# A hybrid decoder layer on one core: eight instead of six fast pairs per pass of the last product, and gate biases that arrive by DMA

## The chip, the cores and the metric

The kernel runs on one core of one Trainium2 chip. The metric is device time in microseconds (us). Before the change three runs took 1597.12, 1597.80 and 1598.16 us; the median is 1597.8. One more execution was recorded by the hardware profiler; every row of a profile in this document comes from such a recording.

Five engines matter: TensorE (PE) multiplies matrices, and its weight loads are listed apart as PEld; VectorE (DVE) and ScalarE (ACT) work element by element; GpSimd (POOL) is nearly unused; SyncE (SP) issues the DMA transfers. Each engine takes its own instructions in order.

## The reference

The reference is one layer of a decoder trunk over 256 tokens of width 2048, in f32. From the conditioning vector c it forms six modulation vectors:

```python
mod = jax.nn.silu(c) @ w_ada[l] + b_ada[l]
shift1, scale1, gate1, shift2, scale2, gate2 = jnp.split(mod[:, None, :], N_MOD, axis=-1)
h = rms_norm(x, norm1_gain[l]) * (1 + scale1) + shift1
x = x + gate1 * mixing_sublayer(h, ...)      # three token mixers, one output product
h = rms_norm(x, norm2_gain[l]) * (1 + scale2) + shift2
x = x + gate2 * swiglu(h, w_ffn_in[l], w_ffn_out[l])
```

`swiglu` splits `h @ w_ffn_in` into two halves of width 5632, takes `silu(gate) * up`, and multiplies by `w_ffn_out` (5632 x 2048). This product with `w_ffn_out` is the last product of the kernel. The change touches it and the biases `b_ada` of the two gates.

## The kernel before

**Three matmuls per product.** Every f32 factor is split into a high part (a cast to fp32r, written `hi`, `whi`) and a low part (the rest, `lo`, `wlo`). `mm3` (L163) issues hi x hi, hi x lo and lo x hi into one PSUM bank; each is a matmul of 128x128 by 512 columns. ACT casts the high part and DVE subtracts for the low part. For weights that happens in `load_weights` (L146, L158, L159) and in `load_pair` (L1269, L1276, L1277), out of pools of four buffers each: `raw`, `whi`, `wlo`. One buffer holds two 128-row chunks of 512 columns.

**Units and pairs.** The feed-forward network runs in 11 units of 512 columns. `act[e]` holds the high and low part of unit e, transposed: four chunks of 128 rows (k) by 256 tokens. The last product runs over 44 chunks, which is 22 pairs of chunks, by four column blocks of 512. Pass one (`OUT_A`) forms column blocks 0 and 1 over all 22 pairs. Pass two (`OUT_B`) forms blocks 2 and 3 over a part of the pairs, and `block` calls add the rest, with the last block's end split by token half so that little is left behind the final matmul.

**Ordinary and fast pairs.** For a pair, two chunks by two token halves meet two chunks by two column blocks: eight block products, 24 matmuls. `fast_products` (L1284 and on) can instead form a pair by seven block products (a Strassen-like scheme, 21 matmuls). It then needs sums of the left factors (`sums_of_unit`, L1427 and on; `sums_of`, L1251) and of the weights (`load_pair`: one 1024-wide and five 512-wide subtractions more than for an ordinary pair, L1277 and L1280, four of them in the buffers with the tags AR0 and AR1). Seven products land in eight banks: the four accumulators and four shared ones, which are added to the accumulators after the last fast pair of a pass (`merge`, L1311, out of the sums L1352 to L1355). Before the change six pairs of each pass are fast: pairs 8 to 13, whose left factors belong to units 4, 5 and 6. The tuples `OUT_A` and `OUT_B` list the order as (pair, fast); `hooks` says before which position the sums of a unit are written out, and at which position `flush` completes all background work.

**The gates.** A modulation vector is a product with `w_ada` that DVE forms: for each of 16 chunks and two halves a tile of 128x1024 is loaded (L375, SP), and one instruction adds weight times silu(c) to an accumulator (`ada_mac`: L286 for the first chunk, a multiplication; L288 for the others). `rows_of` (L965 and on) then adds the bias to row 0 of each quarter of the accumulator (DMA L970, DVE add L971), splits the quarters into high and low parts (L980, L981) and multiplies them by a matrix of ones on PE (L985, L986), which sums over the partitions and leaves the gate in every row. This is background work: a generator from which `tick` takes a step at a given rate per two chunks of a `block`, `RATE_FFN` = 0.65 in the feed-forward network and 2.5 in the last product. Gate 2 starts with unit 8. A multiply-add is issued three steps after its load, and is queued on DVE behind the last weight split that the code has written out by then (`issue_after`); within a block that is the block's last split, so these instructions run in bursts towards the end of a block. Gate 1 is formed in the same way during the mixing sub-layer, in tiles with the tags T4 and T5.

**What sets the order.** The code is written in one order, and a scheduler sorts the instructions of each engine by priority and by the time at which its own model finds them ready. Work inside `prio()` counts as 4000 instructions earlier; all weight loads and splits are such work, and the sums of left factors are not. On the chip each engine then keeps the order it was given. A tile with one buffer (AR0, AR1, KC, ada) is free for its next owner only when every reader of the old contents is done.

Of the kernel before, what the change touches and what calls it, by code (L numbers as in the profile page):

```python
# [10 lines left out]
F32 = mybir.dt.float32  # L11
F32R = mybir.dt.float32r
# [5 lines left out]
P = 128  # L18
# [14 lines left out]
RATE_IN, RATE_MID, RATE_FFN = 0.8, 0.6, 0.65  # L33
RATE_OUT = 2.5
LOOK = 3
# [41 lines left out]
def trunk(ctx: ExitStack, tc: tile.TileContext, I, out):  # L77
# [205 lines left out]
    def ada_mac(acc, raw, k):  # L283
        c = csil[:, k : k + 1]
        if k == 0:
            nc.vector.tensor_scalar(acc, raw, c, None, op0=ALU.mult)  # L286
        else:
            nc.vector.scalar_tensor_tensor(acc, raw, c, acc, op0=ALU.mult, op1=ALU.add)  # L288
# [69 lines left out]
    def mac():  # L358
        acc, j, k, raw, done = macs.pop(0)
        with tc.issue_after(state["split"].ins):  # L360
            ada_mac(acc[j], raw, k)
        if done is not None:
            after.append(done)

    def ada_segment_steps(acc, seg, done):


        for k in range(KC):
            for j in range(2):
                while len(macs) >= len(ring["tags"]):  # L370
                    mac()
                raw = araw([P, 2 * NB])
                c0 = seg * D + j * 2 * NB
                with prio():
                    nc.sync.dma_start(raw, w_ada[k * P : (k + 1) * P, c0 : c0 + 2 * NB])  # L375
                macs.append((acc, j, k, raw, done if (k, j) == (KC - 1, 1) else None))
                yield
# [587 lines left out]
    def rows_of(name, seg, acc):  # L965

        quarters = [a[:, c : c + NB] for a in acc for c in (0, NB)]
        for j, q in enumerate(quarters):
            br = scr([1, NB])
            nc.sync.dma_start(br, I["b_ada"][:, seg * D + j * NB : seg * D + (j + 1) * NB])  # L970
            nc.vector.tensor_add(q[0:1, :], q[0:1, :], br)  # L971
            yield
# [21 lines left out]
    def background():  # L994
        for seg in (SEG_SHIFT2, SEG_GATE1, SEG_SCALE2):
            if seg == SEG_GATE1:
                acc = [S(f"T{4 + j}", [P, 2 * NB]) for j in range(2)]
                yield from ada_segment_steps(acc, seg, rows_of("gate1", seg, acc))
# [241 lines left out]
    def gate2_bg():  # L1240
        acc = halves(S("ada", [P, D]))
        yield from ada_segment_steps(acc, SEG_GATE2, rows_of("gate2", SEG_GATE2, acc))
        yield from last_macs()
# [180 lines left out]
    CUT = KF - 14  # L1424
    w_fo = I["w_ffn_out"]
    out_sums = {}

    def sums_of_unit(n):
# [6 lines left out]
        hi, lo = (S(f"H{2 + 2 * n + i}", [P, 4, 2, P], F32R) for i in range(2))  # L1435
        nc.scalar.copy(hi, sf)
        nc.vector.tensor_tensor(lo, sf, hi.bitcast(F32), op=ALU.subtract)
        for m in range(2):
            out_sums[2 * e + m] = [(hi[:, j, m, :], lo[:, j, m, :]) for j in range(4)]
# [3 lines left out]
    hooks = {at: (lambda n=n: sums_of_unit(n)) for n, at in enumerate((1, 2, 4))}  # L1443
    hooks[7] = flush
# [7 lines left out]
    REST = 2 * len(OUT_B)  # L1452
    block(o[0], act_at, w_fo, REST, KF, 2 * NB, go_on=True, seeded=True)
# [5 lines left out]
    block(pss, act_at, w_fo, REST, CUT, n * NB, go_on=True, more=True, seeded=True)  # L1459
# [42 lines left out]
```

## Time and profile before

| | |
|---|---|
| median of three runs | 1597.8 us |
| the profiled execution, its time | 1597.22 us |
| its span, first to last instruction | 1595.4 us |
| granted TensorE clock | 1.000 |
| PE / DVE / ACT / POOL busy | 1582.0 / 1275.5 / 837.6 / 5.3 us |
| DMA, mean | 248 GB/s |
| last product, first matmul to last | 1352.9 to 1591.0 us |

Times within the profile count from the first instruction. A row of a timeline gives start, duration, engine, source line, operation, what is written and read (buffer numbers left out), the shape, and in brackets how long the engine had been idle before and whom it had waited for. "L166" is line 166 of the kernel; the lines of a helper are shared by all who call it. Neighbouring rows of one kind can be merged. A matmul's listed duration is longer than its distance to the next, because matmuls are pipelined; a few matmul records can be missing. A row of a group gives the busy time in all, the mean of one in nanoseconds, and the idle time before.

### The profile page before, as it was taken

The numbers are of one execution on the slowest core, as the hardware profiler recorded it, in microseconds if no ns is written. First come the engines' busy times: TensorE is split into PE (matmuls) and PEld (weight loads), VectorE is DVE, ScalarE is ACT, GpSimd is POOL, SyncE is SP. The second block draws the span as 40 slices with busy tenths as digits, with TensorE's granted clock in tenths as the row PEclk, the third lists the DMA queues.
The fourth block names the chain that finished last, engine by engine and source line by source line (L and its number), as shares of the span: only waits on it lengthen the run. The fifth ranks groups of instructions, "written<-read, shape, count | busy, mean of one in ns | idle before, by whom it ended". The sixth has DMA issues, their size and how long they took to land.

```text
span 1595.4 us, 20167 instructions
## 1 busy us (share of the span) xinstructions
PE 1582.0 (99%) x7272; PEld 1308.2 (82%) x7272; DVE 1275.5 (80%) x1523; ACT 837.6 (53%) x1184; POOL 5.3 (0%) x14
## 2 busy tenths in 40 slices
PE   8999999999999999999999999999999999999998
PEld 7878888888888888888887888888888888778887
DVE  6889995888878787878756688888887677988884
ACT  5654449775754434444446655555454443554552
POOL 1000000000000000000000000000000000000000
PEclk9999999999999999999999999999999999999999
DMA  9999997667778889989766466556657889667664
GB/s 339 365 326 320 332 302 245 214 189 257 247 258 280 297 301 314 311 289 310 228 192 210 149 196 195 192 184 193 205 183 226 281 302 314 203 196 225 212 204 140
DMA packets 194596, 395.97 MB, mean 248 GB/s; under 512 B 12914, under 2 KB 27928, under 8 KB 194496
## 3 DMA queue, kind: packets, MB, share of 16 engines
q1 hardware_dynamic: 194096, 394.60, 75.0%
q8 instruction: 57, 0.93, 0.2%
q14 instruction: 43, 0.35, 0.1%
q10 hardware_dynamic: 176, 0.07, 0.0%
q0 software_dynamic: 224, 0.01, 0.0%
HBM read 392.53 MB, written 2.10 MB: 247 GB/s over the span
## 4 chain that ended last, share of the span: by engine, by line
PE 85%; DMA 5%; DVE 5%; ACT 3%; issue 2%; SPq 0%; ACTq 0%; DVEq 0%
PE acc L166 21%; PE acc L165 21%; PE acc L164 20%; PE misc L164 6%; PE misc L166 6%; PE misc L165 6%; DVE wlo L159 1%; ACT whi L158 1%; DMA AR<-w_ada 1%; DVE ada L288 1%; DMA raw<-w_br_gla 1%; DMA raw<-w_ffn_out 1%; PE acc L434 1%; DMA raw<-w_in 1%; PE misc L800 1%
## 5 line engine op out<-in xcount | busy, mean ns | idle before, releaser
L158 ACT CAST whi<-raw 128x1024 fp32r<-128x1024 f32 x362 | 368.6, 1022 | 412.2 <-PE acc L166 264.9
L159 DVE TENSOR_TENSOR wlo<-raw,whi 128x1024 fp32r<-128x1024 f32 x362 | 425.6, 1183 | 186.0 <-ACT whi L158 184.4
L164 PE MATMUL acc<-whi,H 128*128 128x512 f32 x1308 | 511.9, 392 | 1.2 <-ACT H L446 0.8
L165 PE MATMUL acc<-wlo,H 128*128 128x512 f32 x1308 | 510.9, 391 | 0.8 <-DVE wlo L159 0.7
L166 PE MATMUL acc<-whi,H 128*128 128x512 f32 x1308 | 509.8, 390 | 0.4 <-DVE H L453 0.4
L166 PEld LDWEIGHTS acc<-whi,H 128*128 128x128 f32 x1308 | 245.3, 188 | 52.9 <-DVE H L453 1.6
L164 PEld LDWEIGHTS acc<-whi,H 128*128 128x128 f32 x1308 | 245.5, 188 | 52.3 <-ACT H L446 1.3
L165 PEld LDWEIGHTS acc<-wlo,H 128*128 128x128 f32 x1308 | 245.7, 188 | 51.3 <-DVE wlo L159 1.7
L1276 ACT CAST whi<-raw 128x1024 fp32r<-128x1024 f32 (+1 forms) x184 | 179.2, 992 | 134.5 <-PE acc L166 68.0
L1277 DVE TENSOR_TENSOR wlo<-raw,whi 128x1024 fp32r<-128x1024 f32 (+1 forms) x184 | 205.2, 1145 | 19.8 <-ACT whi L1276 18.8
L164 PE MATMUL misc<-whi,H 128*128 128x512 f32 x246 | 96.1, 391 | 0.0
L165 PE MATMUL misc<-wlo,H 128*128 128x512 f32 x246 | 95.8, 389 | 0.0
L166 PE MATMUL misc<-whi,H 128*128 128x512 f32 x246 | 95.8, 389 | 0.0
L164 PE MATMUL acc<-whi,A 128*128 128x512 f32 x222 | 87.1, 394 | 0.5 <-ACT whi L1276 0.4
L165 PE MATMUL acc<-wlo,A 128*128 128x512 f32 x222 | 86.7, 390 | 0.8 <-DVE wlo L159 0.8
L166 PE MATMUL acc<-whi,A 128*128 128x512 f32 x216 | 84.3, 390 | 0.0
L288 DVE SCALAR_TENSOR_TENSOR ada<-AR,csil,ada 128x1024 f32<-128x1024 f32 x59 | 74.8, 1278 | 3.6 <-DMA AR<-w_ada 3.6
L165 PEld LDWEIGHTS misc<-wlo,H 128*128 128x128 f32 x246 | 46.2, 188 | 9.7 <-DVE wlo L1277 0.2
L166 PEld LDWEIGHTS misc<-whi,H 128*128 128x128 f32 x246 | 46.2, 188 | 9.5
L164 PEld LDWEIGHTS misc<-whi,H 128*128 128x128 f32 x246 | 46.2, 188 | 9.5
L164 PEld LDWEIGHTS acc<-whi,A 128*128 128x128 f32 x222 | 41.7, 188 | 9.6 <-ACT whi L1276 1.1
L165 PEld LDWEIGHTS acc<-wlo,A 128*128 128x128 f32 x222 | 41.7, 188 | 9.6 <-DVE wlo L159 1.1
(428 smaller groups left out, 1927.6 us busy)
## 6 DMA issues: line engine op xcount, KB each, us to landing
raw<-w_in SPq DMA_DIRECT2D x205, 512.0 KB, 4.8
raw<-w_ffn_in SPq DMA_DIRECT2D x176, 512.0 KB, 4.2
raw<-w_ffn_out SPq DMA_DIRECT2D x88, 512.0 KB, 4.8
AR<-w_ada SPq DMA_DIRECT2D x79, 512.0 KB, 5.1
raw<-w_out SPq DMA_DIRECT2D x32, 512.0 KB, 4.8
KC<-w_ada SPq DMA_DIRECT2D x30, 512.0 KB, 6.2
OS<-w_ada SPq DMA_DIRECT2D x16, 512.0 KB, 6.9
KD<-w_ada SPq DMA_DIRECT2D x16, 512.0 KB, 5.8
```

What stands on the lines that cost most here:

```text
L158: state["cast"] = nc.scalar.copy(hi[:, :n, :], raw[:, :n, :])
L159: state["split"] = nc.vector.tensor_tensor(lo[:, :n, :], raw[:, :n, :], hi[:, :n, :].bitcast(F32), op=ALU.subtract)
L164: nc.tensor.matmul(ps, lh, rh, start=start, stop=False, skip_group_check=seeded)
L165: nc.tensor.matmul(ps, lh, rl, start=False, stop=False, skip_group_check=seeded)
L166: state["mm"] = nc.tensor.matmul(ps, ll, rh, start=False, stop=stop, skip_group_check=seeded)
L288: nc.vector.scalar_tensor_tensor(acc, raw, c, acc, op0=ALU.mult, op1=ALU.add)
L434: state["warm"] = nc.tensor.matmul(ps, ones_r, wide, start=True, stop=True)
L800: nc.tensor.matmul(ps[:n, t * N_GLA + h, :].rearrange("p (s l) -> p s l", l=L), at(f, h, t)[:, :n], odd(at(f, h, t)), start=True, stop=True,)
L1276: nc.scalar.copy(hi[:, :n, :], src)
L1277: state["split"] = nc.vector.tensor_tensor(lo[:, :n, :], src, hi[:, :n, :].bitcast(F32), op=ALU.subtract)
```

## The change

- **Eight fast pairs per pass.** Pairs 6 to 13 are fast in both passes, so unit 3 is added to units 4, 5 and 6. Pass one has five ordinary pairs first, then fast and ordinary ones in turn, and one ordinary pair behind. Pass two grows from 14 to 16 pairs; in it pairs 7 and 8, and pairs 10 and 11, are fast ones directly behind one another. The `block` calls after pass two lose the two pairs that pass two gained, and the last token-half part has 12 chunks instead of 14.
- **Room for the sums.** A fast pair does not read the second token half of its first chunk, so the first of the four sums of each unit is written over it, in the unit's own `act` tiles. The other three sums of units 3, 4 and 5 lie in three quarters of the tiles H2 to H7, and those of unit 6 in the last quarter of all six. The copies and subtractions that write them are cut into two pieces, for unit 6 into four.
- **When the sums are written out.** Before positions 0, 2, 6 and 9 of pass one, instead of 1, 2 and 4; `flush` moves from position 7 to 4. `LOOK`, the number of pairs that pass one asks for ahead, goes from 3 to 2.
- **Gate biases.** The accumulators of gates 1 and 2 are set to zero on POOL, and the bias row is written into row 0 by DMA before the first multiply-add. That one becomes a multiply-add like the others. The four bias DMAs, the four adds and four turns of waiting in `rows_of` go.
- **Rate.** `RATE_FFN` goes from 0.65 to 0.75.

```diff
-RATE_IN, RATE_MID, RATE_FFN = 0.8, 0.6, 0.65
+RATE_IN, RATE_MID, RATE_FFN = 0.8, 0.6, 0.75
-LOOK = 3
+LOOK = 2
-OUT_UNITS = (4, 5, 6)
-OUT_A = tuple((p, 0) for p in range(7)) + tuple(x for i in range(6) for x in ((8 + i, 1), ((7, 14, 15, 16, 17, 18)[i], 0))) + (
-    (19, 0), (20, 0), (21, 0))
-OUT_B = ((0, 0), (1, 0)) + tuple(x for i in range(6) for x in ((8 + i, 1), (2 + i, 0)))
+OUT_UNITS = (3, 4, 5, 6)
+OUT_A = tuple((p, 0) for p in range(5)) + tuple(x for i in range(8) for x in ((6 + i, 1), ((5, *range(14, 21))[i], 0))) + ((21, 0),)
+OUT_B = tuple((p, int(6 <= p < 14)) for p in (0, 1, 6, 2, 7, 8, 3, 9, 4, 10, 11, 5, 12, 14, 13, 15))
...
-        if k == 0:
+        if k == 0 and zero:
             nc.vector.tensor_scalar(acc, raw, c, None, op0=ALU.mult)
...
+    def biased(acc, seg):
+        for j, a in enumerate(acc):
+            nc.gpsimd.memset(a, 0.0)
+            with prio():
+                nc.sync.dma_start(a[0:1, :], I["b_ada"][:, seg * D + j * 2 * NB : seg * D + (j + 1) * 2 * NB])
+        return acc
...
-        for j, q in enumerate(quarters):
-            br = scr([1, NB])
-            nc.sync.dma_start(br, I["b_ada"][:, seg * D + j * NB : seg * D + (j + 1) * NB])
-            nc.vector.tensor_add(q[0:1, :], q[0:1, :], br)
-            yield
...
-    CUT = KF - 14
+    CUT = 2 * len(OUT_B)
+    rooms = [S(f"H{2 + j}", [P, 4, 2, P], F32R) for j in range(6)]
...
-        hi, lo = (S(f"H{2 + 2 * n + i}", [P, 4, 2, P], F32R) for i in range(2))
-        nc.scalar.copy(hi, sf)
-        nc.vector.tensor_tensor(lo, sf, hi.bitcast(F32), op=ALU.subtract)
+        homes = []
+        for part in range(2):
+            own = act[e][part][:, 0:4:2, P:T]
+            if n < 3:
+                rest = [(rooms[2 * n + part][:, 0:3], slice(1, 4))]
+            else:
+                rest = [(rooms[2 * j + part][:, 3:4], slice(1 + j, 2 + j)) for j in range(3)]
+            homes.append([(own, 0)] + rest)
+        for part in range(2):
+            for (dst, c), (hi, _) in zip(homes[part], homes[0]):
+                if part == 0:
+                    nc.scalar.copy(dst, sf[:, c])
+                else:
+                    nc.vector.tensor_tensor(dst, sf[:, c], hi.bitcast(F32), op=ALU.subtract)
...
-    hooks = {at: (lambda n=n: sums_of_unit(n)) for n, at in enumerate((1, 2, 4))}
-    hooks[7] = flush
+    hooks = {at: (lambda n=n: sums_of_unit(n)) for n, at in enumerate((0, 2, 6, 9))}
+    hooks[4] = flush
...
-    REST = 2 * len(OUT_B)
-    block(o[0], act_at, w_fo, REST, KF, 2 * NB, go_on=True, seeded=True)
+    block(o[0], act_at, w_fo, CUT, KF, 2 * NB, go_on=True, seeded=True)
...
-    block(pss, act_at, w_fo, REST, CUT, n * NB, go_on=True, more=True, seeded=True)
```

More of the change, by code (lines that the diff above doesn't have):

```diff
@@ L281, in trunk, with ada_mac @@
     w_ada = I["w_ada"]
-    def ada_mac(acc, raw, k):
+    def ada_mac(acc, raw, k, zero=True):
         c = csil[:, k : k + 1]
-        if k == 0:
+        if k == 0 and zero:
             nc.vector.tensor_scalar(acc, raw, c, None, op0=ALU.mult)
@@ L375, in ada_segment_steps @@
                     nc.sync.dma_start(raw, w_ada[k * P : (k + 1) * P, c0 : c0 + 2 * NB])
-                macs.append((acc, j, k, raw, done if (k, j) == (KC - 1, 1) else None))
+                macs.append((acc, j, k, raw, done if (k, j) == (KC - 1, 1) else None, zero))
                 yield
@@ L996, in background @@
             if seg == SEG_GATE1:
-                acc = [S(f"T{4 + j}", [P, 2 * NB]) for j in range(2)]
-                yield from ada_segment_steps(acc, seg, rows_of("gate1", seg, acc))
+                acc = biased([S(f"T{4 + j}", [P, 2 * NB]) for j in range(2)], seg)
+                yield from ada_segment_steps(acc, seg, rows_of("gate1", seg, acc), False)
             else:
@@ L1240, in gate2_bg @@
     def gate2_bg():
-        acc = halves(S("ada", [P, D]))
-        yield from ada_segment_steps(acc, SEG_GATE2, rows_of("gate2", SEG_GATE2, acc))
+        acc = biased(halves(S("ada", [P, D])), SEG_GATE2)
+        yield from ada_segment_steps(acc, SEG_GATE2, rows_of("gate2", SEG_GATE2, acc), False)
         yield from last_macs()
```

14 lines of the change are left out of this document (10 added, 4 removed).

## The prediction

> **What bounds the kernel now.** I read the page first, then busy time by stretch, then the timelines of TensorE (PE), VectorE (DVE) and ScalarE (ACT) in the last product, then groups and waits.
>
> ```profile
> span 1595.4 us, 20167 instructions
> PE 1582.0 (99%) x7272; PEld 1308.2 (82%) x7272; DVE 1275.5 (80%) x1523; ACT 837.6 (53%) x1184; POOL 5.3 (0%) x14
> ```
>
> ```profile
> 1240.00:1350.00 110.00, 110.00 (x495) 91.24 (x494) 83.78 (x78) 47.16 (x50) 0.00 (x0) 1.00 0.87 294
> 1310.00:1320.00 10.00, 10.00 (x49) 8.35 (x49) 7.65 (x9) 4.13 (x5) 0.00 (x0) 1.00 1.00 363
> 1410.00:1540.00 130.00, 130.00 (x575) 107.47 (x574) 112.17 (x127) 69.90 (x74) 0.00 (x0) 1.00 0.67 211
> ```
>
> After each stretch come PE, weight load, DVE, ACT and POOL, busy time and count, then granted clock, DMA share and GB/s. From 1410 to 1540 PE starts 575 matmuls in 130 us, one per 0.226 us, at clock 1.00, without a gap. A matmul's own 0.39 us overlaps the next, so 0.226 is what a removed one is worth while PE never waits. DVE is 86% busy there: close behind.
>
> The last product starts at 1352.89, and only its beginning loses PE time:
>
> ```profile
> 1352.89 0.39 PE L164 MATMUL acc<-whi,A 128*128 128x512 f32 x1
> ...
> 1358.33 1.04 PE L1115 MATMUL misc<-ident,scr 128*128 128x128 f32 x8
> 1359.13 0.48 PE L164 MATMUL acc<-whi,A 128*128 128x512 f32 x1
> ```
>
> ```profile
> 1371.49 0.39 PE L164 MATMUL acc<-whi,A 128*128 128x512 f32 x1
> 1372.70 0.39 PE L985 MATMUL misc<-T,ones_r 128*128 128x256 f32 x1 [0.82 <-ACT T L980]
> ...
> 1395.28 0.28 PE L986 MATMUL misc<-T,ones_r 128*128 128x256 f32 x1
> 1395.40 0.40 PE L164 MATMUL acc<-whi,A 128*128 128x512 f32 x1
> ```
>
> ```profile
> 1402.75 0.40 PE L165 MATMUL acc<-wlo,A 128*128 128x512 f32 x1
> ```
>
> At 1371.49 the next start comes after 1.21 us instead of 0.23: 0.98 lost, waiting for the cast of a gate row. The first fast pair (seven block products, 21 matmuls) starts at 1395.40. The second matmul after it starts at 1402.75, 22 matmuls and four gate-row matmuls (0.12 each, 1395.28 to 1395.40) later: 22 x 0.226 + 0.48 = 5.45 us were due, 7.35 passed, 1.90 lost. Together 2.9 us.
>
> **The change part by part.**
>
> *Four more fast pairs.* An ordinary pair is 24 matmuls, a fast one 21; six become eight in each of two passes: 4 x 3 = 12 matmuls less, 12 x 0.226 = **-2.7 us**. The blocks that follow lose the pairs that pass two gains, one for one. The Trainium skill ("TensorE: Matmul & The Clock Gate", section "Back-to-back issue gap") gives about 131 ns per 512-column matmul in a sustained stream; by it the saving would be 1.6 us and the whole sum below 1.1 us less of a gain. The trace, with 226 ns, does not agree, and the trace is used.
>
> *What a fast pair costs DVE.* One steady period (a fast and an ordinary pair), and the slack at its end:
>
> ```profile
> 1409.20 1.05 ACT L1276 CAST whi<-AR 128x1024 fp32r<-128x1024 f32 x1 [1.97 <-DVE AR L1280]
> ```
>
> ```profile
> 1408.40 0.69 DVE L1280 TENSOR_TENSOR AR<-raw,AR 128x512 f32<-128x512 f32 x1
> 1410.28 1.23 DVE L1277 TENSOR_TENSOR wlo<-AR,whi 128x1024 fp32r<-128x1024 f32 x1 [1.19 <-ACT whi L1276]
> 1411.42 3.49 DVE L1277 TENSOR_TENSOR wlo<-raw,whi 128x1024 fp32r<-128x1024 f32 x3
> 1414.83 0.69 DVE L1280 TENSOR_TENSOR AR<-raw,raw 128x512 f32<-128x512 f32 x1
> 1415.43 0.68 DVE L1280 TENSOR_TENSOR AR<-raw 128x512 f32<-128x512 f32 x1
> ...
> 1420.33 1.23 DVE L1277 TENSOR_TENSOR wlo<-AR,whi 128x1024 fp32r<-128x1024 f32 x1 [1.20 <-ACT whi L1276]
> ```
>
> ```profile
> 1496.47 0.39 PE L164 MATMUL acc<-whi,A 128*128 128x512 f32 x1
> 1497.80 1.23 DVE L1277 TENSOR_TENSOR wlo<-AR,whi 128x1024 fp32r<-128x1024 f32 x1 [0.93 <-ACT whi L1276]
> 1500.10 0.39 PE L165 MATMUL acc<-wlo,H 128*128 128x512 f32 x1
> ```
>
> Start to start a 1024-wide subtraction takes 1.14 us (1410.28 to 1411.42), a 512-wide one 0.60 (1414.83 to 1415.43). An ordinary pair is two wide ones, 2.3 us; a fast pair three wide and five narrow, 6.4. So the period is 8.7 us of DVE work plus a hole of 1.2 in which DVE waits for the cast at 1409.20: 10.05 (1410.28 to 1420.33). PE needs 45 x 0.226 = 10.17. The last split of the fast pair at 1496.47 ends at 1499.03 and is read at 1500.10: 1.07 us of slack, regained at 0.12 per period.
>
> *Gate 2 earlier, biases by DMA.*
>
> ```profile
> 1345.11 2.47 DVE L288 SCALAR_TENSOR_TENSOR ada<-AR,csil,ada 128x1024 f32<-128x1024 f32 x2
> ...
> 1355.46 1.28 DVE L288 SCALAR_TENSOR_TENSOR ada<-AR,csil,ada 128x1024 f32<-128x1024 f32 x1
> ...
> 1369.19 1.28 DVE L288 SCALAR_TENSOR_TENSOR ada<-KC,csil,ada 128x1024 f32<-128x1024 f32 x1 [0.17 <-DMA KC<-w_ada]
> ```
>
> ```profile
> L971 DVE TENSOR_TENSOR ada<-ada,scr 1x512 f32<-1x512 f32 x4 | 2.6, 673 | 0.0
> L286 DVE TENSOR_SCALAR T<-AR,csil 128x1024 f32<-128x1024 f32 x1 | 0.7, 747 | 0.0
> L605 POOL CAST KC<-T x1: 1037/1037/1037, 245.9 to 245.9; 128x1024 uint8<-128x1024 f32 x1
> SPq L970 <- PE misc L938: 6.3, 1, 6.3
> ```
>
> By the code, units 8 to 10 have 48 ticks. At 0.65 they give 31 of the 35 steps that issue all 32 gate multiply-adds, so four are left over and run up to 1369.19; at 0.75 they give 36, and the last comes in the burst that runs from 1345.11 to 1355.46, some 14 us earlier. The four bias adds (2.6 us of DVE) go, and eight turns of waiting become four; in return two first steps per gate turn from 0.75 to 1.28. Net 1.6 us less of DVE per gate, twice. The 0.98 us stall goes, since the cast it waited for stood behind these. Next behind it are the splits for the fast pair. Cover for the higher rate: weights take 524 KB per 12 matmuls (193 GB/s), the gate 0.65 or 0.75 of that, so 318 becomes 338 GB/s, under the 363 of the 1310 row; DVE goes from 76% to about 81%. I take 0. Without that cover each 4% of missing bandwidth over 110 us would cost 4.4.
>
> The four memsets: the nearest POOL row is 1.04 us; POOL is idle, 0. The new bias DMAs (two per gate for four) wait on SP for the memset, with all weight and gate loads behind them. The old bias DMA once held SP 6.3 us, yet PE shows no stall beside it: four split buffers of 12 matmuls are 10.9 us of cover. I take 0; beyond the cover each us would cost one.
>
> *First fast pair, position 5 instead of 7.* DVE from 1353.1 to its last split: eight ordinary splits 9.1, the last unit's four narrow operations 2.4, one gate step 1.2, two sums 7.4 (below), eight gate-row splits of 0.34 2.7, fast pair 6.4: 29.2, so 1382.3. PE gets there at 1352.9 + 0.8 (the eight transposes from 1358.33) + 5 x 24 x 0.226 + 16 x 0.12 = 1382.7 and reads the last split 3.6 later: 4.0 us for holes. So the 1.90 goes as well: **-2.9** together. Bounds: 0 (both stalls stay) to -2.9.
>
> *Two sums of left factors among the fast pairs* (hooks 6 and 9; all three stood ahead of them before).
>
> ```profile
> 1372.13 1.21 DVE L1432 TENSOR_TENSOR AR<-A,T 128x1024 f32<-128x1024 f32 x1
> 1381.30 1.21 DVE L1437 TENSOR_TENSOR H<-AR,H 128x1024 fp32r<-128x1024 f32 x1
> ```
>
> ```profile
> L1251 DVE TENSOR_TENSOR AR<-AR,AR 128x256 f32<-128x256 f32 x6 | 2.5, 416 | 0.0
> L981 DVE TENSOR_TENSOR T<-ada,T 128x256 fp32r<-128x256 f32 x8 | 3.3, 418 | 0.7 <-ACT T L980 0.7
> ```
>
> Each is one wide add 1.14, four of 256 columns at some 0.34 start to start, and a subtraction in pieces, 1.2 to 1.4: 3.7 and 3.8 us. Its buffers AR0 and AR1 are those of the fast pairs' differences, so it must fit between two fast pairs, and whoever needs AR0 next waits. The wide add fits the 1.2 hole. The first then adds 2.6: 10.05 + 2.6 - 10.17 = 2.5 late, less 1.07 of slack, 1.4 us. The second finds some 0.2 of slack: 2.7 - 0.1 - 0.2, about 2.3. **+3.7**. Bounds: 0 (all in holes) to twice 9.3 (rival 2). I take 3.7, since the steady period with its hole is the nearest row.
>
> *Two places in pass two where fast follows fast.* Ordinary, fast, fast is 66 x 0.226 = 14.9 us of PE and 2.3 + 2 x 6.4 = 15.1 of DVE, 17.5 if both holes stay: 0 to 1.5 late after slack, at each. The second pair's weights are loaded well before, so the holes should fill: **+0.3** of 0 to 3.0.
>
> *No cost:* the last merge moves behind pass one, two adds before its bank is wanted two ordinary pairs (10.8 us) later; the end after the last matmul is unchanged; LOOK only delays what is asked for by one pair, which two buffered pairs cover.
>
> **Sum:** -2.7 - 2.9 + 3.7 + 0.3 = -1.6. The profiled execution took 1597.22 (its span 1595.4 and 1.8 around it), 0.6 under the median of 1597.8: 1595.6 on its scale, **1596.2 us** as a median.
>
> **Rivals.**
> 1. *The late sums fit.* For: DVE has 14% free from 1410 to 1540, and the adds are short. Against: the same buffers, and a hole at one place only. If each costs 0.2: -2.7 - 2.9 + 0.4 = -5.2, 1592.6.
> 2. *Slower: a sum's chain holds the buffers.* Before, one ran from 1372.13 to 1382.5, 10.4 us, with other work in between. A fast pair's first difference comes at 1414.83. If the chain starts only there, behind the three splits, the next fast pair is 10.4 late, 9.3 after slack. One such place and one normal one: -2.7 - 2.9 + 9.3 + 2.3 + 0.3 = +6.3, 1604.1. It decides from 8.5 lost in all, 4.2 at each: such chains starting at 1409.7 on the clock of the steady period above. Against: nothing forces other work in between.
> 3. *The change does not clear the start.* The first fast pair comes two pairs earlier with less time before it, and both stalls stay in another place: -2.7 + 4.0 = +1.3, 1599.1.
>
> **How the numbers follow.** Forecast 0.42, rival 1 0.33, rival 2 0.15, rival 3 0.10. 0.2% is 3.2 us, about what a measurement tells from no change. Faster: rival 1 and the forecast's best edge, 0.36; slower: rival 2, 0.15; the rest 0.49. The range goes from just under rival 1, 1592.4, to 1601.2, half the way into rival 2, and leaves out about 2 in 10.
>
> **What would show it.** PE at 12 matmuls less, DVE's last gate step before 1358, no gate-row wait near 1371, PE gaps only in the fast pairs behind hooks 6 and 9, 1 to 3 us each, and none in pass two. Wrong: gaps at the first fast pair, AR0's next writer far behind its normal place, or PE waits in the units before, from the higher gate rate.

## The result, and the profile after

The changed kernel takes 1607.32 us (median of four runs, 1606.98 to 1608.74) against 1597.98 us for the kernel before beside it; the ratio is 1.0057, 95% interval 1.0042 to 1.0072. It is slower by 9.3 us, above the predicted range. The profiled execution took 1608.74 us, 11.5 more than that of before. Its first half ran 2.3 us later up to the start of the feed-forward network (874.0 against 871.7 us); over all the profiles of this study, which have the first half in common but for gate 1's bias, that start lies between 871.4 and 875.7, so scatter alone can make it; whether gate 1's bias has a part in it is taken up with kernel 4.

The head of the page of the changed kernel:

```profile
span 1607.0 us, 20214 instructions
PE 1585.8 (99%) x7260; PEld 1306.6 (81%) x7260; DVE 1293.2 (80%) x1551; ACT 843.6 (52%) x1199; POOL 9.1 (1%) x18
```

PE has 12 matmuls less than before, as the change says, but needs more time. Busy time by stretch says where (first the changed kernel, then one row of the kernel before; columns as in the prediction):

```profile
1240.00:1350.00 110.00, 109.23 (x489) 90.16 (x489) 83.22 (x77) 44.69 (x49) 0.00 (x0) 1.00 0.89 304
1340.00:1365.00 25.00, 19.71 (x79) 15.50 (x78) 18.60 (x17) 8.72 (x9) 0.00 (x0) 0.93 0.87 294
```

```profile
1340.00:1365.00 25.00, 25.00 (x116) 20.78 (x115) 20.87 (x20) 10.47 (x12) 0.00 (x0) 1.00 0.95 322
```

In the 25 us around the end of unit 10 and the start of the last product PE starts 79 matmuls; before, 116. The groups of waits of PE from 1340 to 1400 name one large one, and it is at a gate row:

```profile
PE misc L988 <- ACT T L983: 4.5, 1, 4.5
PE acc L164 <- DVE wlo L158: 0.8, 1, 0.8
```

Followed back, from the timelines of PE, ACT, DVE and SP's queue in turn, all of the changed kernel:

```profile
1348.34 0.50 PE L164 MATMUL acc<-wlo,H 128*128 128x512 f32 x1 [0.77 <-DVE wlo L158]
...
1361.10 0.58 PE L988 MATMUL misc<-T,ones_r 128*128 128x256 f32 x1 [4.53 <-ACT T L983]
1361.47 0.63 PE L163 MATMUL acc<-whi,A 128*128 128x512 f32 x1
1361.90 0.63 PE L164 MATMUL acc<-wlo,A 128*128 128x512 f32 x1
```

```profile
1349.89 1.05 ACT L157 CAST whi<-raw 128x1024 fp32r<-128x1024 f32 x1 [1.54 <-DMA raw<-w_ffn_in]
...
1360.64 0.41 ACT L983 CAST T<-ada 128x256 fp32r<-128x256 f32 x1 [5.12 <-DVE ada L288]
```

```profile
1350.97 1.23 DVE L158 TENSOR_TENSOR wlo<-raw,whi 128x1024 fp32r<-128x1024 f32 x1 [1.37 <-ACT whi L157]
1352.11 1.28 DVE L288 SCALAR_TENSOR_TENSOR ada<-AR,csil,ada 128x1024 f32<-128x1024 f32 x1
...
1359.32 1.28 DVE L288 SCALAR_TENSOR_TENSOR ada<-AR,csil,ada 128x1024 f32<-128x1024 f32 x1 [1.26 <-DMA AR<-w_ada]
...
1361.65 1.28 DVE L1402 TENSOR_TENSOR scr<-scr,acc 128x512 f32<-128x512 f32 x2
1362.85 1.28 DVE L288 SCALAR_TENSOR_TENSOR ada<-KC,csil,ada 128x1024 f32<-128x1024 f32 x1
```

```profile
1342.28 0.34 SPq L383 DMA_DIRECT2D AR<-w_ada  x1
1342.67 0.43 SPq L145 DMA_DIRECT2D raw<-w_ffn_in  x1
1343.41 9.18 SPq L1272 DMA_DIRECT2D raw<-w_ffn_out  x4
1353.42 0.34 SPq L383 DMA_DIRECT2D AR<-w_ada  x1
```

The same cast in the kernel before:

```profile
1372.24 0.41 ACT L980 CAST T<-ada 128x256 fp32r<-128x256 f32 x1 [0.86 <-DVE ada L971]
```

Read from the bottom: a gate load goes out on SP at 1342.28, when the multiply-add that read the old contents of its buffer (started at 1340.96) has ended; the last weight load of unit 10 follows right behind it, at 1342.67. The cast and the split of these weights wait for them (1349.89 and 1350.97). The multiply-add at 1352.11 stands behind that split, and when it has read its buffer the next gate load can go out, at 1353.42. (Four loads of weights for the last product, which wait for free buffers, stand between the two gate loads; the last of them went out at 1352.22.) The multiply-add of that load waits 1.26 us for it and starts at 1359.32; the cast of the first gate row follows, and then the row's matmul.

In PE's queue that matmul is now the first instruction of the stretch: it stands ahead of the first matmul of the last product (1361.47). Before, 79 matmuls of the last product stood ahead of it, and it started 19.8 us into the product (1352.89 to 1372.70, the rows of the prediction). The last multiply-add came earlier by 6.3 us (1362.85 for 1369.19), or 8.6 without the 2.3 us of the first half. The row's cast came 11.6 us earlier (1360.64 for 1372.24), but its matmul was due 15.3 us earlier (1356.57 for 1371.88, each the start less the wait). The difference, 3.7 us, and the 0.82 us that PE waited there before make the 4.53.

Not all the work behind the row was ready. The multiply-add at 1359.32 stands ahead of L1402 on DVE too, the multiplication that reads unit 10's last product out of its banks, and the thirteenth matmul of the last product needs one of these banks: in kernel 2 below, where the row is out of the way, that matmul waits 2.70 us for L1402. Counted from the time at which the product was due, this multiplication (L1399 in the kernel before and kernel 3) starts 1.4 us behind in the kernel before, 4.5 to 5.3 in the five profiles at rate 0.75 that have gate 2 (the changed kernel, 2, 3, 5 and 6), 1.4 to 2.9 in the others at 0.65, and 0.3 us ahead in kernel 7, which has no gate 2.

### The profile page after: what moved, and what is told of

The parts are those of the page before. It is cut to its first block, busy times and chain, and to the rows that moved or that the text cites. A ratio compares the mean times of both kernels' runs of the same rounds, so it can differ in the third digit from the quotient of the medians.

```text
span 1607.0 us, 20214 instructions
## 1 busy us (share of the span) xinstructions
PE 1585.8 (99%) x7260; PEld 1306.6 (81%) x7260; DVE 1293.2 (80%) x1551; ACT 843.6 (52%) x1199; POOL 9.1 (1%) x18
## 4 chain that ended last, share of the span: by engine, by line
PE 80%; DVE 8%; DMA 6%; ACT 3%; issue 3%; SPq 0%; ACTq 0%; DVEq 0%
PE acc L165 20%; PE acc L164 20%; PE acc L163 20%; PE misc L164 5%; PE misc L165 5%; PE misc L163 5%; DVE wlo L1280 3%; DMA raw<-w_ffn_in 2%; DVE AR L1283 1%; DMA raw<-w_ffn_out 1%; DVE ada L288 1%; DVE wlo L158 1%; DMA KC<-w_ada 1%; ACT whi L157 1%; PE acc L442 1%
## 5 line engine op out<-in xcount | busy, mean ns | idle before, releaser
L157 ACT CAST whi<-raw 128x1024 fp32r<-128x1024 f32 x358 | 364.4, 1021 | 410.9 <-PE acc L165 246.0
L163 PE MATMUL acc<-whi,A 128*128 128x512 f32 x216 | 85.3, 395 | 0.0
L165 PE MATMUL acc<-whi,A 128*128 128x512 f32 x208 | 81.6, 392 | 0.0
L1279 ACT CAST whi<-AR 128x1024 fp32r<-128x1024 f32 x32 | 33.7, 1052 | 53.5 <-DVE AR L1283 48.1
L1280 DVE TENSOR_TENSOR wlo<-AR,whi 128x1024 fp32r<-128x1024 f32 x32 | 39.2, 1224 | 17.5 <-ACT whi L1279 17.5
```

The source lines that it names most:

```text
L157: state["cast"] = nc.scalar.copy(hi[:, :n, :], raw[:, :n, :])
L163: nc.tensor.matmul(ps, lh, rh, start=start, stop=False, skip_group_check=seeded)
L165: state["mm"] = nc.tensor.matmul(ps, ll, rh, start=False, stop=stop, skip_group_check=seeded)
L1279: nc.scalar.copy(hi[:, :n, :], src)
L1280: state["split"] = nc.vector.tensor_tensor(lo[:, :n, :], src, hi[:, :n, :].bitcast(F32), op=ALU.subtract)
```

## What the loss adds up to

For the stretches from unit 10 on I compare the distance between matmul starts with 0.226 us each (0.12 for a gate-row matmul) and call the rest lost. In passes one and two I sum this over pairs; for unit 10 its whole duration stands, 44.4 us where nothing is lost. Matmuls are counted against the kernel before, at 0.226 us. The last column but one is the sum, less that of the kernel before; the last is the ratio of the runs, which include the profiled one, as us of 1598.

| kernel | unit 10 | pass one | pass two | matmuls | sum | measured |
|---|---|---|---|---|---|---|
| before | 44.4 | 4.1 | 0.0 | 0 | 0 | 0 |
| changed | 50.7 | 7.3 | 3.0 | -2.7 | +9.8 | +9.1 |
| 1 changed, rate 0.65 | 44.4 | 9.8 | 3.4 | -2.7 | +6.4 | +6.6 |
| 2 changed, 8 turns | 44.4 | 12.1 | 4.4 | -2.7 | +9.7 | +8.5 |
| 3 before, rate 0.75 | 45.5 | 7.3 | 0.0 | 0 | +4.3 | +3.4 |
| 4 before, bias by DMA | 44.4 | 3.2 | 0.2 | 0 | -0.7 | +1.4 |
| 5 changed, pass two spaced | 48.6 | 6.8 | 0.1 | -2.7 | +4.3 | +5.0 |
| 6 changed, sums in KC | 49.6 | 8.4 | 3.7 | -2.7 | +10.5 | +11.7 |
| 7 changed, no gate 2 | 44.4 | 4.3 | 3.1 | -2.7 and -1.9 | -1.3 | -0.8 |
| 8 seven and eight | 44.4 | 5.4 | 4.7 | -2.0 | +4.0 | +0.5 |
| 9 as 1 and 5, 16 turns | 44.4 | 11.9 | 0.2 | -2.7 | +5.4 | +4.5 |
| 10 pass two alone | 44.4 | 4.8 | 0.0 | -1.4 | -0.7 | -2.1 |
| 11 and bias by DMA, 16 turns | 44.4 | 6.7 | 0.0 | -1.4 | +1.2 | -1.1 |
| 12 the same, 12 turns | 44.4 | 4.7 | 0.0 | -1.4 | -0.8 | -1.3 |

The -1.9 of kernel 7 are the 16 gate-row matmuls of gate 2. The sums come from one execution each, the measured column from 4 to 11; an interval is 1.4 to 2.4 us to each side. With the exception of 8 and, less so, of 4 and 11 the two agree within about 1.5 us. Kernel 8 was profiled in its slowest execution, 1604.6 us for a median of 1599.5, and kernel 4 in its second fastest, 1598.1 for 1601.5. A figure of one execution scatters: kernel 5 has the changed kernel's code up to pass two, yet loses 4.2 us in unit 10 and not 6.3.

The changed kernel loses 6.3 us in unit 10, 3.1 more than before in pass one and 3.0 in pass two, for 2.7 gained.

## The experiments

### 1 and 2: where the gate rows stand against the gate steps

From the changed kernel:

```diff
-RATE_IN, RATE_MID, RATE_FFN = 0.8, 0.6, 0.75
+RATE_IN, RATE_MID, RATE_FFN = 0.8, 0.6, 0.65
```

> The changed kernel with RATE_FFN back at 0.65, nothing else. Theory R (the rate): six gate loads per block instead of five stand in SP's queue ahead of weight loads and starve the splits of the last units, and the gate's first row product is queued on PE ahead of the last product; the unit before the last product took 6.3 us longer than before, and 1.4 us more went at half the clock behind it. Then this run gains 7.7 us: about 1599.6. Theory T (the turns: the four waiting turns and adds that went from rows_of let the row product be queued too early): only the 1.2 us weight wait goes, about 1606.

1605.19 us, ratio 1.0041 (1.0026 to 1.0056). Unit 10 is back at 44.4 us, but only 2.6 us come back by the runs, whose intervals overlap (3.4 by the table): pass one loses 2.5 more. So the 7.7 us of theory R did not come, and theory T, whose time is near, did not expect unit 10 to recover. The first gate row still waits, now inside pass one:

```profile
1366.48 0.39 PE L988 MATMUL misc<-T,ones_r 128*128 128x256 f32 x1 [1.83 <-ACT T L983]
```

and the fast pair at position 5 loses 1.98 us, which it did not in the changed kernel.

From the changed kernel, in `rows_of`:

```diff
-        for _ in range(4):
+        for _ in range(8):
```

> The changed kernel with eight turns of waiting in rows_of instead of four, the rate left at 0.75. Theory R: the weights starve as before and the gate's last steps come as late; the row product moves 24 matmuls back in PE's queue, but it still stands ahead of its cast, so part of its 4.5 us wait goes: 1604 to 1607. Theory T: the wait and the slow clock go, 1601.5.

1607.07 us, 1.0053 (1.0038 to 1.0068): no difference. The row wait before the product is gone and unit 10 takes 44.4 us, but the thirteenth matmul of the product now waits 2.70 us for a bank that L1402 on DVE has to read first, again behind a gate multiply-add that waited for its load:

```profile
1361.56 0.47 PE L163 MATMUL acc<-whi,A 128*128 128x512 f32 x1 [2.70 <-DVE scr L1402]
```

```profile
1358.39 1.28 DVE L288 SCALAR_TENSOR_TENSOR ada<-AR,csil,ada 128x1024 f32<-128x1024 f32 x1 [1.05 <-DMA AR<-w_ada]
```

Pass one loses 12.1. Unit 10's time and the losses of the two passes together come to 60.9 us, against 61.0 in the changed kernel. To move the rows alone moves the loss. The upper end of theory R's time came, without the row wait that it gave as the reason.

### 3 and 4: one part of the change in the kernel before

From the kernel before:

```diff
-RATE_IN, RATE_MID, RATE_FFN = 0.8, 0.6, 0.65
+RATE_IN, RATE_MID, RATE_FFN = 0.8, 0.6, 0.75
```

> The kernel before with RATE_FFN 0.75 and nothing else. Theory R: slower by 4 us or more, 1602 to 1606, with a PE wait at the first row product or in the last unit. Theory T: four adds and four turns still delay the row product, so within 1 us of 1598.

1601.99 us, 1.0021 (1.0011 to 1.0031): the higher rate alone costs 3.4 us (1.8 to 5.0). That is less than the 4 or more of theory R, and theory T's "within 1 us" is out. PE's timeline has two new waits at the start of the last product, the first again at the thirteenth matmul:

```profile
1359.97 0.47 PE L164 MATMUL acc<-whi,A 128*128 128x512 f32 x1 [2.78 <-DVE scr L1399]
...
1366.10 0.39 PE L985 MATMUL misc<-T,ones_r 128*128 128x256 f32 x1 [1.56 <-ACT T L980]
```

From the kernel before: memset and bias DMA for both gates, the four bias steps of `rows_of` go and four turns stay; rate, orders and sums are as before. For gate 2:

```diff
-        acc = halves(S("ada", [P, D]))
-        yield from ada_segment_steps(acc, SEG_GATE2, rows_of("gate2", SEG_GATE2, acc))
+        acc = biased(halves(S("ada", [P, D])), SEG_GATE2)
+        yield from ada_segment_steps(acc, SEG_GATE2, rows_of("gate2", SEG_GATE2, acc), False)
```

> The kernel before with the gate biases put in the accumulators by DMA (memset on POOL, four adds and four turns gone), rate 0.65. Theory R: within 1 us of 1598, at best 1 us faster (the 0.98 us wait for the row cast). Theory T: slower by 3 to 6 us, with a PE wait of several us at the first row product.

1601.54 us, 1.0009 (1.0000 to 1.0018). The first row now has 58 matmuls of the product ahead of it and waits 1.33 us for its cast, and the loss of the first fast pair falls from 1.89 to 0.23. By the runs the bias DMA brings nothing and may cost up to 2.9 us; the one profile, of one of its shortest executions, is 0.7 us better than that of before. The several us of theory T did not come. Part of any cost may lie ahead of unit 0, which the table leaves out: in the eight profiles with gate 1's bias by DMA the feed-forward network starts at 873.8 us in the median (872.8 to 874.5), in the six without at 872.3 (871.4 to 875.7). That is within the scatter, and not settled.

### 5: pass two without neighbouring fast pairs

From the changed kernel:

```diff
-OUT_B = tuple((p, int(6 <= p < 14)) for p in (0, 1, 6, 2, 7, 8, 3, 9, 4, 10, 11, 5, 12, 14, 13, 15))
+OUT_B = tuple((p, int(6 <= p < 14)) for p in (0, 1, 6, 2, 7, 3, 8, 4, 9, 5, 10, 14, 11, 15, 12, 16, 13, 17))
```

> The changed kernel with pass two in the order 0 1 6f 2 7f 3 8f 4 9f 5 10f 14 11f 15 12f 16 13f 17 (f is fast): an ordinary pair between any two fast ones, the same matmuls. Theory P (fast behind fast overloads DVE): the 3.0 us that PE lost in pass two (1.06 at the first place, 1.27 at the second, 0.23 behind) go, -2.5 to -3. Rival (the loss comes from the room that the sums share, or from reading it): it stays, within 0.7 us of the changed kernel.

1604.32 us, 1.0031 (1.0017 to 1.0044). The theory held. In the changed kernel PE waited twice in each of the two places in pass two:

```profile
1515.29 0.50 PE L163 MATMUL acc<-whi,H 128*128 128x512 f32 x1 [0.20 <-ACT whi L1279]
1516.23 0.51 PE L163 MATMUL misc<-whi,A 128*128 128x512 f32 x1 [0.21 <-ACT whi L1279]
...
1541.90 0.50 PE L163 MATMUL acc<-whi,H 128*128 128x512 f32 x1 [0.34 <-ACT whi L1279]
1542.85 0.49 PE L163 MATMUL misc<-whi,A 128*128 128x512 f32 x1 [0.22 <-ACT whi L1279]
```

The idle time listed is only part of it: by the starts 1.06 and 1.27 us are lost at these two, and 0.23 at the last fast pair. With an ordinary pair between, PE never waits in pass two; busy time by stretch of kernel 5:

```profile
1485.00:1575.00 90.00, 90.00 (x398) 74.38 (x397) 80.46 (x93) 49.23 (x53) 0.00 (x0) 1.00 0.67 213
```

398 matmuls in 90 us are 0.226 each. So eight fast pairs cost nothing in pass two, but neighbouring ones do: the 3.0 us of the changed kernel become 0.1. (The rest of the 4.1 us by which this kernel is faster than the changed one lies ahead of pass two, in code that the edit does not touch.)

### 6: another buffer for the sums

From the changed kernel, in `sums_of_unit`:

```diff
-        full = S("AR0", [P, 4, T])
+        full = S("KC", [P, 4, T])
```

> The changed kernel with the first buffer of the sums of left factors under the tag KC instead of AR0, which the fast pairs' weight differences use. Theory B (the buffer): a late sum makes the next fast pair wait for AR0, so the two losses in pass one (1.3 us in pair 7, 2.3 in pair 9) fall by more than half, -2 us. Rival D (DVE's time): the operations are the same and DVE has 1.2 us free per period, so they stay within 0.7 us.

1610.35 us, 1.0073 (1.0058 to 1.0088): no gain. The two late sums of the changed kernel show up on PE thus:

```profile
1408.55 0.50 PE L163 MATMUL misc<-whi,H 128*128 128x512 f32 x1 [0.34 <-ACT whi L1279]
...
1429.62 0.50 PE L164 MATMUL misc<-wlo,A 128*128 128x512 f32 x1 [0.60 <-DVE wlo L1280]
1431.38 0.50 PE L163 MATMUL misc<-whi,H 128*128 128x512 f32 x1 [0.56 <-ACT whi L1279]
```

By the starts, 1.30 us at the fast pair behind hook 6 and 2.31 behind hook 9. With the first buffer out of AR0 they are 2.02 and 2.45. It is not this buffer that makes them; theory B fell. In DVE's timeline of the changed kernel the wide addition of the second of these sums, at 1417.31, lies where DVE otherwise waits 1.2 us for a cast, so that the split behind it does not wait; the rest of the sum is extra work:

```profile
1417.31 1.22 DVE L1436 TENSOR_TENSOR AR<-T,T 128x1024 f32<-128x1024 f32 x1
1418.59 1.23 DVE L1280 TENSOR_TENSOR wlo<-AR,whi 128x1024 fp32r<-128x1024 f32 x1
1419.73 4.09 DVE L1280 TENSOR_TENSOR wlo<-raw,whi 128x1024 fp32r<-128x1024 f32 x4
```

### 7: the changed kernel without gate 2

From the changed kernel:

```diff
-            bg.append(gate2_bg())
+            acc2 = S("ada", [P, D])
+            nc.gpsimd.memset(acc2, 1.0)
+            state["gate2"] = [acc2[:, c : c + NB] for c in range(0, D, NB)]
```

> The changed kernel without gate 2: its 32 loads and multiply-adds and its row products are left out, and ones stand in its place. Theory G (gate 2's late steps cause the loss at the start): the unit before the last product takes 44.4 us again, positions 0 to 6 of pass one lose under 0.5 us together, while the losses of pairs 7 and 9 and of pass two stay: about 1597 (6.3 + 3.4 us of losses and 1.9 of row products less). Rival (the sums and the two pairs fewer ahead of the first fast pair overload DVE anyway): 1.5 us or more is lost at position 5.

Ones stand in the place of gate 2, so the output is no longer the layer's; the run serves for its times alone. 1597.87 us, 0.9995 (0.9986 to 1.0004): 9.9 us less than the changed kernel by the ratios, 1.9 of them the 16 row matmuls that are not there. Unit 10 takes 44.4 us, positions 0 to 6 of pass one lose nothing, the fast pair at position 5 among them; the late sums (1.35 and 2.29) and pass two (3.06) lose what they lost. Busy time by stretch at the same place as above:

```profile
1340.00:1365.00 25.00, 25.00 (x116) 20.78 (x115) 16.84 (x20) 11.78 (x15) 0.00 (x0) 1.00 0.58 189
```

So everything lost in unit 10 and in the first seven pairs is lost to gate 2, as theory G had it; which of its loads, multiply-adds and rows does it, this run cannot tell, since all of them go.

### 8: seven fast pairs in pass one, eight in pass two

From the kernel before: pass two as in kernel 5, the room for the sums as in the changed kernel, gate 2's bias by DMA with four turns, and in pass one

```diff
-OUT_UNITS = (4, 5, 6)
+OUT_UNITS = (4, 5, 6, 3)
-OUT_A = tuple((p, 0) for p in range(7)) + tuple(x for i in range(6) for x in ((8 + i, 1), ((7, 14, 15, 16, 17, 18)[i], 0))) + (
-    (19, 0), (20, 0), (21, 0))
+OUT_A = tuple((p, 0) for p in range(6)) + ((7, 0),) + tuple(x for i in range(6) for x in ((8 + i, 1), (14 + i, 0))) + (
+    (20, 0), (6, 1), (21, 0))
-    hooks = {at: (lambda n=n: sums_of_unit(n)) for n, at in enumerate((1, 2, 4))}
+    hooks = {at: (lambda n=n: sums_of_unit(n)) for n, at in enumerate((1, 2, 4, 18))}
```

> A version put together from what the runs showed: rate 0.65, LOOK 3, pass one starts as before (six fast pairs of units 4 to 6 behind seven ordinary ones, hooks 1, 2, 4, flush 7) and has a seventh fast pair (pair 6) behind a gap of two ordinary ones, with the sums of unit 3 in it; pass two has eight fast pairs with an ordinary one between any two; the bias by DMA is kept for gate 2 alone. Nine matmuls less (2.0 us), no late sum in the dense part, none of pass two's loss: 1596 plus or minus 1 on the scale where the kernel before takes 1598; if the gate rows wait as in the fourth run, 1 more.

1599.53 us, 1.0003 (0.9994 to 1.0013): nine matmuls less, and no gain, where 1596 was expected. A fast pair as the last but one of pass one puts the merge of the shared banks and the first part of the output on DVE right ahead of the splits that pass two needs:

```profile
1484.31 1.29 DVE L1428 TENSOR_TENSOR A<-A,scr 128x512 f32<-128x512 f32 x2
1485.52 3.49 DVE L1286 TENSOR_TENSOR wlo<-raw,whi 128x1024 fp32r<-128x1024 f32 x3
```

```profile
1486.79 0.80 PE L165 MATMUL misc<-wlo,A 128*128 128x512 f32 x1 [2.35 <-DVE wlo L1286]
```

### 9: rate, order of pass two and place of the rows, together

From the changed kernel, with `OUT_B` as in kernel 5, and

```diff
-RATE_IN, RATE_MID, RATE_FFN = 0.8, 0.6, 0.75
+RATE_IN, RATE_MID, RATE_FFN = 0.8, 0.6, 0.65
...
-        for _ in range(4):
+        for _ in range(16 if name == 'gate2' else 4):
```

> The changed kernel with three edits: rate 0.65, pass two with an ordinary pair between every two fast ones (18 pairs, eight of them fast), and 16 turns of waiting for gate 2 in place of 4, which puts its first gate-row matmul about four pairs later in TensorE's queue (924 instead of 1020 matmuls of the product behind it). Theory that the start is lost because the gate-row matmuls stand in the queue ahead of the last gate step: the waits of 1.99 and 0.91 us of the run at rate 0.65 go, and so does most of the 3.39 us of pass two; what is left are the two late sums, 3.6 us, and the 12 matmuls saved, -2.7: 1599.5 us, within 0.2% of the kernel before. Rival, that at rate 0.65 the fast pair at position 5 itself comes too early for VectorE: a loss of about 2 us at position 5 stays whatever the turns, 1601.5 us.

1603.24 us, 1.0028 (1.0017 to 1.0038). The theory of the place alone fell, and the rival held: the row waits shrink to under 0.9 us each, but the first fast pair and the ordinary pair behind it lose 3.0 and 2.9. PE and DVE there:

```profile
1395.33 0.73 PE L163 MATMUL acc<-whi,A 128*128 128x512 f32 x2 [1.02 <-ACT whi L1279]
1396.95 0.79 PE L164 MATMUL acc<-wlo,A 128*128 128x512 f32 x1 [0.77 <-DVE wlo L1280]
1397.54 0.63 PE L165 MATMUL acc<-whi,A 128*128 128x512 f32 x1
```

```profile
1364.00:1398.00 34.00, 29.92 (x126) 22.46 (x125) 33.74 (x51) 16.79 (x25) 0.00 (x0) 0.98 0.56 185
```

DVE is busy for 33.74 of 34 us there. At rate 0.65 the end of gate 2, its rows, two sums, the splits and the first fast pair at position 5 fill DVE, at both places of the rows that were tried (kernels 1 and 9); at 0.75 the burst comes sooner and stops unit 10 or the start of the product instead.

### 10 to 12: what is left of the change

Kernel 10 is the kernel before with gates, rate, `LOOK` and `OUT_A` as they were, the room for the sums and the later merge as in the changed kernel, and

```diff
-OUT_UNITS = (4, 5, 6)
+OUT_UNITS = (4, 5, 6, 3)
-OUT_B = ((0, 0), (1, 0)) + tuple(x for i in range(6) for x in ((8 + i, 1), (2 + i, 0)))
+OUT_B = tuple((p, int(6 <= p < 14)) for p in (0, 1, 6, 2, 7, 3, 8, 4, 9, 5, 10, 14, 11, 15, 12, 16, 13, 17))
-    hooks = {at: (lambda n=n: sums_of_unit(n)) for n, at in enumerate((1, 2, 4))}
+    hooks = {at: (lambda n=n: sums_of_unit(n)) for n, at in enumerate((1, 2, 4, 19))}
```

> The kernel before with pass two alone changed: eight fast pairs of 18 with an ordinary one between every two, left factors for the two more made from unit 3 at position 19 of pass one; gates, rate, and the order of pass one as before. Six matmuls fewer than before. Theory that more fast pairs cost nothing where each has an ordinary one beside it, and where no sum falls among fast pairs that leave VectorE no room: 6 x 0.226 = 1.4 us less, ratio 0.9991. Rival, that any sum late in pass one costs 1.3 to 2.3 us of TensorE as those of hooks 6 and 9 did: ratio 0.9999 to 1.0006.

1597.16 us over 11 runs, 0.9987 (0.9979 to 0.9996), beside 1599.05 us for the kernel before in the same session. This is the one version here that beats both kernels: 2.1 us (0.6 to 3.4), where six matmuls are 1.4. Its matmul count on the page, and busy time by stretch in pass two:

```profile
PE 1580.4 (99%) x7266; PEld 1306.9 (82%) x7266; DVE 1287.5 (81%) x1547; ACT 842.2 (53%) x1195; POOL 5.7 (0%) x14
```

```profile
1476.00:1568.00 92.00, 92.00 (x407) 76.18 (x406) 80.44 (x93) 50.74 (x53) 0.00 (x0) 1.00 0.65 211
```

The fourth unit's sums, written out at position 19, where only ordinary pairs are left, cost PE nothing: the theory held, and its rival fell.

In kernels 11 and 12 gate 2's bias comes by DMA in addition, with 16 or 12 turns:

```diff
-        acc = halves(S("ada", [P, D]))
-        yield from ada_segment_steps(acc, SEG_GATE2, rows_of("gate2", SEG_GATE2, acc))
+        acc = biased(halves(S("ada", [P, D])), SEG_GATE2)
+        yield from ada_segment_steps(acc, SEG_GATE2, rows_of("gate2", SEG_GATE2, acc), False)
...
-        for _ in range(4):
+        for _ in range(16 if name == 'gate2' else 4):
```

> As the run with pass two alone changed, and gate 2's bias put in its accumulators by DMA, with 16 turns of waiting in place of the four bias steps and four turns (first gate-row matmul with 930 matmuls of the product behind it, 953 before). Theory that the bias adds are worth what TensorE waits for them, at most the 0.98 us of the gate row of before: 0 to 1 us less than the run without it. Rival, that the earlier first row waits for the last gate step, as in the changed kernel: a wait at a gate-row matmul, 1 to 2 us more.

> The same with 12 turns: the first gate-row matmul has 954 matmuls of the product behind it, 24 more than with 16 turns, so it stands one pair earlier in TensorE's queue. Theory that the place of the row matmuls against the last gate step decides: if a row wait shows with 16 turns, it is longer here by up to one pair (24 x 0.226 = 5.4 us); if none shows with either, the times are equal within 0.1%. Rival, that the place does not matter: equal times and equal waits.

1598.15 us, 0.9993 (0.9985 to 1.0002), and 1597.82 us, 0.9992 (0.9983 to 1.0001). The two are equal, as the last expectation allows if no row waits long, and neither is better than kernel 10. No row waits more than about 1 us in either. The bias adds were worth nothing that can be measured.

## Why the prediction was wrong

**The 12 matmuls, -2.7.** Right: 7272 became 7260, and without waits one costs 0.226 us (kernels 5 and 10).

**Both start stalls go, -2.9.** This is the step that failed, by way of "I take 0" for the gate at the higher rate. Things were costed apart that meet on DVE and on PE. The prediction followed the last gate step and found it "some 14 us earlier"; it came 6 to 9 earlier, since each gate load waits for its buffer until a multiply-add, itself queued behind a weight split, has read it. Nor did the prediction ask what stands behind the gate steps on DVE at the end of unit 10: L1402, before which the product does not get its banks, and the cast of the first row. And it counted the turns of waiting that go only as DVE time and never asked where the row matmuls then stand in PE's queue. They moved by 79 matmuls, ahead of the last product, farther than the producer; the rate alone moves them by 48 (kernel 3), the bias steps alone by 21 (kernel 4).

In place of -2.9 the runs show +6.3 in unit 10 (1.03 at a weight split, 4.69 ahead of the row's matmul, the rest spread). Up to the first fast pair 3.1 us are lost in pass one, 3.0 of them at positions 0 to 3, where 4.1 were lost before. That is 5.3 us more in place of 2.9 less: about 8.2 of the 10.9 us by which the forecast of the change (-1.6, measured +9.3) is off. All of it is gone with gate 2 (kernel 7), and it stays when the rows alone are moved (kernel 2). No rival named this: rival 2, nearest in time with 1604.1, put the loss at the late sums.

**Cover for the higher rate.** The sum was made of bandwidth (338 of 363 GB/s) and of DVE's share. On the average neither was short: from 1240 to 1350 the changed kernel moved 304 GB/s, with DVE busy for 83.22 of 110 us. That short stretches of full DMA had no part in the late loads is not shown. The rate alone costs 3.4 us in the kernel before (kernel 3). What the average of 81% hid is that the gate's multiply-adds come in a burst at the end of a block, ahead of splits and of the multiplication that the next product waits for.

**The first fast pair at position 5.** The budget of 29.2 us allowed one gate step behind 1353.1. At 0.75 one step is left behind the start of the product, and the pair does lose nothing, but PE had waited before it, so that DVE had more time than the budget gave it. At 0.65 it loses 1.98 and 3.03 (kernels 1 and 9), with DVE full. So there is no rate of the two at which the start is free, and rival 3 was right in kind: the stalls stay in another place. It priced them at 2.9 over the forecast, as if they could not grow.

**Two late sums, +3.7.** Right, each by itself: 1.4 and 2.3 predicted, 1.30 and 2.31 measured. It is not luck: kernels 2, 5 and 7 lose 1.3 to 1.4 and 2.3 there too (kernel 1 only 0.3 at the first). The reason was right as well: the wide add lies in the hole and the rest is late. That the buffers matter, the premise of rival 2 and the point against rival 1, did not show in kernel 6, which moved one of the two buffers only.

**Fast behind fast, +0.3 of 0 to 3.0.** Mis-sized: 2.3 at the two places and 3.0 in all of pass two, at the upper bound, which is the other 2.7 us of the miss. One of the two holes fills, the other does not, as DVE's order in the changed kernel shows. In the first pair's hole stand two differences of the second pair (1507.57 and 1508.18), and the split at 1508.78 does not wait. The second pair's split waits for its cast as long as that of a lone fast pair, 1.19 us:

```profile
1507.57 0.69 DVE L1283 TENSOR_TENSOR AR<-raw,raw 128x512 f32<-128x512 f32 x1
1508.18 0.69 DVE L1283 TENSOR_TENSOR AR<-raw 128x512 f32<-128x512 f32 x1
1508.78 1.22 DVE L1280 TENSOR_TENSOR wlo<-AR,whi 128x1024 fp32r<-128x1024 f32 x1
...
1515.27 1.23 DVE L1280 TENSOR_TENSOR wlo<-AR,whi 128x1024 fp32r<-128x1024 f32 x1 [1.19 <-ACT whi L1279]
```

With one hole of 1.2 the prediction's own sum is 15.1 + 1.2 - 14.9 = 1.4 a place before slack; 1.06 and 1.27 were lost. That weights were loaded early did not matter for this hole, because that wait is for ACT, which waits for DVE.

**Bias DMAs and memsets, 0.** No cost was found in kernels 11 and 12, and no gain; kernel 4 leaves up to 2.9 us open. LOOK and the later merge were not tried alone.

**The signs named.** 12 matmuls less: seen. Last gate step before 1358: not seen, it came at 1362.85. No row wait near 1371: none there, but a larger one at 1361.10. Gaps at hooks 6 and 9 of 1 to 3 us: seen. No gap in pass two: there were two. The last line of that list, "PE waits in the units before, from the higher gate rate", is what happened.

What stays open: how the loss at the start is shared between ACT's, DVE's and SP's queues, since every attempt to move it moved all three; and whether another place for gate 2, earlier than unit 8, would let the order of pass one with position 5 pay.

## What to carry to other kernels

When background work is shortened or its waiting turns are cut, find both ends: when the last producer runs and where the first consumer now stands in its in-order queue, for there a consumer that moves farther than its producer stops an engine that may have other work ready. Look also at what stands behind the producer on its own engine: here moving the consumer back did not help, because the next product's banks waited behind the same late multiply-add. A busy share below 100% is no cover for work that comes in bursts; budget the stretch between two fixed points (here the last block and the first fast pair), engine by engine. Keep parts of a change apart in the test: here one part, pass two with an ordinary pair between two of the seven-product kind, was worth 2.1 us alone (0.6 to 3.4; its matmuls are 1.4), and was hidden by the rest.

## What was not expected of the hardware

A wait of PE can cost more than its length. Busy time by stretch of the changed kernel during the wait of 4.53 us, in the 3 us behind it, and after that (the granted clock is the third figure from the right):

```profile
1355.00:1361.00 6.00, 1.57 (x7) 0.95 (x6) 4.74 (x5) 0.88 (x3) 0.00 (x0) 0.99 0.94 310
1361.10:1364.10 3.00, 3.00 (x8) 2.42 (x9) 3.00 (x5) 0.89 (x1) 0.00 (x0) 0.50 0.69 234
1364.50:1368.00 3.50, 3.50 (x18) 2.85 (x17) 3.37 (x4) 1.44 (x2) 0.00 (x0) 1.00 0.47 145
```

At clock 0.50 matmuls start 0.43 us apart (1361.47 to 1361.90), and 1.4 us more are lost in the first pair of the product. The Trainium skill ("TensorE: Matmul & The Clock Gate", section "What's actually happening") says that the clock falls to half after about 3.4 us of idleness and comes back after about as long of work; the trace agrees. But shorter waits did it here too. In kernel 8, PE's timeline around a wait of 1.83 us has

```profile
1372.51 0.39 PE L994 MATMUL misc<-T,ones_r 128*128 128x256 f32 x1 [1.83 <-ACT T L989]
...
1374.15 0.63 PE L164 MATMUL acc<-whi,A 128*128 128x512 f32 x1
1374.58 0.63 PE L165 MATMUL acc<-wlo,A 128*128 128x512 f32 x1
```

0.43 us apart again, at a granted clock of 0.50 from 1374.2 to 1377.1, while the same wait of 1.83 us in kernel 1 left the matmuls behind it at their usual distance and the clock at 1.00. So did the wait of 2.78 us in kernel 3, but that of 2.70 us in kernel 2 was followed by a clock of 0.50 from 1362.9 to 1365.7. In kernel 9 several waits of at most 1.02 us close together were followed by it (0.50 from 1397.5 to 1400.0, the row at 1397.54). Two equal waits need not cost the same; what decides it these runs do not show.
